# Two of four weight sums by accumulating DMAs in a Strassen MLP, with four weight buffers and operands read back unsplit

## The chip, the cores and the metric

The kernel runs on one core of a Trainium2 chip. The metric is the device time of one execution in microseconds. The core has a matrix engine (TensorE, PE in the profile), VectorE (DVE), ScalarE (ACT), GpSimd (POOL) and a queue engine (SyncE, SP); DMAs are issued from SP, ACT and POOL and run on 16 DMA engines.

## The reference, cut to what matters

One layer of a hybrid encoder for 512 tokens of width 2048: an input projection, two attention mixers and an output projection, a cross attention to 256 memory tokens, and an MLP. The change is in the MLP and the final norm behind it:

```python
hm = rmsnorm(x, g_mlp[l])                                     # x: 512 x 2048
x = x + jnp.square(jax.nn.relu(hm @ w_up[l])) @ w_down[l]     # w_up: 2048 x 8192, w_down: 8192 x 2048
return rmsnorm(x, g_final)
```

## The kernel before

Everything is float32, split for the matrix engine into a high and a low part (`hi_lo`: ACT casts to float32r, DVE subtracts), so that a product is three matmuls: high by high, high by low, low by high.

**Units.** The two MLP products are cut into 256 units, 128 of up and then 128 of down. A unit is one block of 256 by 512 weights, used as four 128 x 256 pieces a21, a12, a11, a22 in one 128 x 1024 row, against a pair of operand blocks. It is done with Strassen's scheme (Winograd's form): seven products in place of eight. The seven left operands are the three pieces a12, a11, a22 and four sums of pieces; the seven right operands are three blocks of the activations and four sums. Seven products, two halves, three matmuls each: 42 matmuls of 128 x 256 columns a unit (line 310). Eight units that add up in the same seven PSUM banks are a group (up: one g of 16) or a visit (down: one ng for one c, 16 in all); then the seven banks are combined by `gen_up_out` or `gen_down_out`. There are eight banks, so the next group can begin in the one that is free and goes on as the others are released.

**A unit's weights** (`loader`, `strassen_split`, L1450). SP loads the row into one of three `wraw` buffers. POOL forms the four sums in `sring`: one instruction of 512 columns and two of 256. Once the unit two back has been through the matrix engine, `hi_lo` writes the 768 loaded and then the 1024 summed columns into one of two buffers of tile `hl`.

**Up.** The right operands of the eight pairs lie split in tile `big` (`gen_xpair`; the sums of pairs 2 to 7 are made on POOL). At a group's end `gen_up_out` combines the banks on DVE and ACT, applies relu, square and the norm's factor, forms the sums on DVE (four of 512 columns), splits all 3584 columns (two casts of 1792 on ACT, two subtractions of 1792 on DVE) and stores high and low parts from ACT's queue to `tp_dram`: four DMAs of 896 KB.

**Down.** Four chunks c of eight operand pairs, each chunk used by the four ng in turn. `gen_load_t` loads a split pair (1792 KB, ACT's queue) into one of the eight places of `big` when the last visit of the previous chunk has used it, so all eight of a chunk change within one visit. `gen_down_out` adds a visit's banks to the four residual tiles of its ng, part of it on POOL. In the last chunk `gen_square` sums squares in `acc_f` on POOL, and `gen_out` ends the kernel.

**Order of the work.** Each engine runs its own queue in order. The order is fixed at build time by a planner (`Plan`): generators (`spawn`, `until`) issue an instruction when the planner's estimated clocks say that its inputs are ready. All engine instructions of these helpers carry line 139, so they are told apart by tile and shape: on DVE `hl<-wraw,hl 128x768` and `hl<-fb,hl 128x1024` are the two subtractions of a unit's split, on POOL `fb<-wraw 128x512` and `fb<-fb,wraw 128x256` are its sums.

Of the kernel before, what the change touches and what calls it, by code (L numbers as in the profile page):

```python
# [33 lines left out]
FW = 49 * 256  # L34
# [124 lines left out]
def kernel(  # L159
# [32 lines left out]
    wraw = [cp.tile([128, 1024], F32, name=f"wraw{i}") for i in range(3)]  # L192
# [6 lines left out]
    acc_f = cp.tile([128, 512], F32, name="acc_f")  # L199
# [3 lines left out]
    tp_dram = nc.dram_tensor("tp_dram", (32, 128, PAIR), F32, kind="Internal").ap()  # L203
# [5 lines left out]
    cosT = cp.tile([128, 4, 32], F32, name="cosT")  # L209
    sinT = cp.tile([128, 4, 32], F32, name="sinT")  # L210
# [1143 lines left out]
    PRODUCTS = {"p1": (0, 0), "p2": (2, 1), "q4": (1, 6), "p7": (3, 5), "q5": (4, 3), "q6": (5, 4), "p3": (6, 2)}  # L1354
    ORDER = ("p1", "p2", "q4", "p7", "q5", "q6", "p3")
    LAST_ORDER = ("p1", "q6", "p7", "q4", "p2", "q5", "p3")
# [3 lines left out]
    sring = [fslot(4096 + 1024 * i, 1024) for i in range(2)]  # L1360
    gxbufs = Pool([fslot(10496, 2048)])
# [16 lines left out]
    def residual1(n, b):  # L1378

        yield rt(b, res[n])  # L1380
        dve.tensor_tensor(res[n], res[n], b, op=OP.add)
        banks_f.put(b)
        flag.add(("x1", n))
        if n % 2:
            spawn(gen_xpair(n // 2), True)
        yield rt(res[n])
        nc.sync.dma_start(xs_dram[n], res[n])
        while n > 0 and ("sq", 1, n - 1) not in flag:
            yield 0
# [15 lines left out]
    def gen_xpair(q):  # L1405
# [12 lines left out]
        sums([c(4), c(5), c(6), c(7)], c(0), c(1), c(2), c(3), dve if q < 2 else pool)  # L1418
# [6 lines left out]
        flag.add(("xp", q))  # L1425
        if q == 3:
            while not all(("sq", 1, n) in flag for n in range(8)):
                yield 0
            gxbufs.put(fslot(6144, 2048))
# [19 lines left out]

    def strassen_split(i):  # L1450

        raw, s = wraw[i % 3], sring[i % 2]
        hi, lo = HI[units[i].buf], LO[units[i].buf]
        while i == first_s and not all(("xp", q) in flag and ("sq", 1, 2 * q + 1) in flag for q in range(2)):
            yield 0
        while not splits[i - 2].done:
            yield 0
        yield rt(raw)
        two = lambda x: x.rearrange("p (u c) -> p u c", u=2)
        a21 = raw[:, 0:256]  # L1460
# [8 lines left out]
    def strassen_pe(buf, st, pair, first, last, order):  # L1469

        hi, lo = HI[buf], LO[buf]
        for r in order:
            w, t = PRODUCTS[r]
            if first:
                st[r] = take_now(banks_f)[0]
            th, tl = pair[:, 256 * t : 256 * t + 256], pair[:, 1792 + 256 * t : 2048 + 256 * t]
            for e in range(2):
# [4 lines left out]
                smm(out, lo[:, c], th, False, last)  # L1482

    G = fslot(0, 4096)
    HT = fb[:, 6144 : 6144 + 3584].bitcast(F32R)
    CT = fslot(10496, 2048)

    def gen_up_out(g, st):
# [3 lines left out]
        while g == 0 and len(gxbufs) < 2:  # L1492
            yield 0
        while g > 0 and ("t", g - 1) not in flag:
            yield 0
        yield rt(st["p1"])
        act.copy(e1, st["p1"])
        banks_f.put(st["p1"])
        yield rt(e1, st["p2"])
        dve.tensor_tensor(c11, e1, st["p2"], op=OP.add)  # L1500
        banks_f.put(st["p2"])
        yield rt(st["q5"])
        act.copy(e5, st["q5"])
# [31 lines left out]
        for a in (0, 1792):  # L1535
            src = G[:, 512 + a : 2304 + a]
            yield from hi_lo(HT[:, a : a + 1792], src.bitcast(F32R), src)
        for x, o in ((HT.bitcast(F32), 0), (G[:, 512:4096], 1792)):
            yield rt(x)
            for m in range(2):  # L1540
                dst = tp_dram[2 * g + 1 - m][:, o : o + 1792].rearrange("p (r c) -> p r c", r=7)
                nc.scalar.dma_start(dst, x.rearrange("p (r m c) -> p r m c", r=7, m=2)[:, :, m, :])
        flag.add(("t", g))

    def up_units(g):
        st = {}

        def pe(kk):
            def run(buf):
# [12 lines left out]
    def gen_load_t(p):  # L1562

        yield plan.clk["pe"]
        while ("t", p // 2) not in flag:
            yield 0
        dst = big[:, PAIR * (p % 8) : PAIR * (p % 8) + PAIR]
        nc.scalar.dma_start(dst.bitcast(F32), tp_dram[p])
        plan.issue("dma", 100.0, [dst], [], 7000)
        TP[p] = dst  # L1570


    CB = [[[fslot(o + 1024 * m + 512 * t) for t in range(2)] for m in range(2)]
          for o in (0, 2048, 6144, 8192)]
    ev = Pool([fslot(10496 + 512 * i) for i in range(3)])
# [15 lines left out]
    def gen_down_out(c, ng, st, last):  # L1591
# [3 lines left out]
        e1, u2, u3 = yield from take(ev, 3)  # L1595
        side = dve if last else pool
        yield rt(st["p1"])
        act.copy(e1, st["p1"])
        banks_f.put(st["p1"])

        def add(dst, r, op, free=True):
            dve.tensor_tensor(dst, dst, st[r], op=op)
            if free:
                banks_f.put(st[r])

        if last:
            yield rt(st["q6"], e1)
            dve.tensor_tensor(u2, e1, st["q6"], op=OP.subtract)
            banks_f.put(st["q6"])
            side.tensor_tensor(c12, c12, u2, op=OP.add)  # L1610
            yield rt(st["p7"], u2)
            dve.tensor_tensor(u3, u2, st["p7"], op=OP.add)
            banks_f.put(st["p7"])
            side.tensor_tensor(c21, c21, u3, op=OP.subtract)
            side.tensor_tensor(c22, c22, u3, op=OP.subtract)
            yield rt(st["q4"])
            add(c21, "q4", OP.subtract)
            flag.add(("fin", ng, 1, 0))
            side.tensor_tensor(c11, c11, e1, op=OP.add)
            yield rt(st["p2"])  # L1620
            add(c11, "p2", OP.add)
            flag.add(("fin", ng, 0, 0))
            yield rt(st["q5"])
            add(c22, "q5", OP.add, False)
            flag.add(("fin", ng, 1, 1))
            add(c12, "q5", OP.subtract)
            yield rt(st["p3"])
            add(c12, "p3", OP.add)
            flag.add(("fin", ng, 0, 1))
        else:  # L1630
            yield rt(st["p2"], e1)
            add(c11, "p2", OP.add)
            side.tensor_tensor(c11, c11, e1, op=OP.add)
            yield rt(st["q5"])
            add(c12, "q5", OP.subtract, False)
            add(c22, "q5", OP.add)
            yield rt(st["q6"])
            dve.tensor_tensor(u2, e1, st["q6"], op=OP.subtract)
            banks_f.put(st["q6"])
            dve.tensor_tensor(u3, u2, st["p7"], op=OP.add)  # L1640
            banks_f.put(st["p7"])
            add(c21, "q4", OP.subtract)
            yield rt(st["p3"])
            add(c12, "p3", OP.add)
            side.tensor_tensor(c12, c12, u2, op=OP.add)
            side.tensor_tensor(c21, c21, u3, op=OP.subtract)
            side.tensor_tensor(c22, c22, u3, op=OP.subtract)
            for m in range(2):
                for t in range(2):
                    flag.add(("fin", ng, m, t))  # L1650
        ev.put(e1, u2, u3)
# [6 lines left out]
    def down_units(c, ng):  # L1658
        st = {}
        end = c == 3 and ng == 3  # L1660

        def pe(j):
            def run(buf):
                p = 8 * c + j
                if c == 0 and ng == 0 and j == 0:
# [330 lines left out]
```

## Time and profile before

| what | us |
|---|---|
| median of 3 runs | 2441.43 (2439.35 to 2444.55) |
| the profiled execution, its own time | 2439.85 |
| span of its profile | 2438.0 |
| first matmul of the MLP (line 310) | 948.8 |
| last matmul of the MLP | 2409.1 |

The profiled execution is 1.58 us under the median and its own time is 1.85 us over its span. Times below are from the span's start. Busy time is by engine; DMA share is the mean of the 16 DMA engines.

### The profile page before, as it was taken

Reading aid. Unit: us, or ns where it says so; the run is one execution under the profiler, and the core shown is the slowest. Engines: PE = TensorE matmul, PEld = TensorE weight load, DVE = VectorE, ACT = ScalarE, POOL = GpSimd, SP = SyncE. Lnnn points to the kernel's source line nnn. Section 1 sums busy time; section 2 is a strip of 40 time slices with the busy share of each in tenths; the row PEclk is TensorE's granted clock in tenths of the full one; section 3 lists DMA queues with packets and bytes.
Section 4 is the critical chain, followed back from the end, with each engine's and each line's share of the span. In section 5 each row is a group of like instructions: output and inputs, shape, how many; then the busy total and the mean of one; then the engine's idle time right before and its main releaser. Section 6 shows DMA issues by size and latency. Waiting matters only on the chain.

```text
span 2438.0 us, 39899 instructions
## 1 busy us (share of the span) xinstructions
PE 2275.2 (93%) x16024; PEld 2182.4 (90%) x16024; DVE 1683.8 (69%) x2018; ACT 1056.9 (43%) x1481; POOL 1385.2 (57%) x1078
## 2 busy tenths in 40 slices
PE   8999999999999998799999999999799999999995
PEld 8999999998888887799899899898799999999984
DVE  7678434458633667788988988887666666676656
ACT  6543333345432555545545545444333333333432
POOL 3110101021011107888778787786698998998994
PEclk9999999999999999899999999999899999999997
DMA  5332222231343434164464464468737338347322
GB/s 169 102 91 85 72 78 78 68 104 36 104 172 110 154 127 146 61 212 168 149 214 156 163 206 151 166 204 326 263 97 305 136 113 328 113 145 289 103 79 87
DMA packets 144090, 361.45 MB, mean 148 GB/s; under 512 B 10241, under 2 KB 75793, under 8 KB 139553
## 3 DMA queue, kind: packets, MB, share of 16 engines
q1 hardware_dynamic: 79072, 239.76, 29.6%
q10 hardware_dynamic: 64752, 119.06, 13.4%
q8 instruction: 125, 2.05, 0.4%
q14 instruction: 61, 0.49, 0.1%
q0 software_dynamic: 80, 0.08, 0.0%
HBM read 291.76 MB, written 67.11 MB: 147 GB/s over the span
## 4 chain that ended last, share of the span: by engine, by line
PE 45%; POOL 26%; DVE 14%; issue 8%; DMA 5%; ACT 1%; SPq 0%; DVEq 0%; ACTq 0%; POOLq 0%
PE bank L305 30%; POOL fb L139 26%; PE bank L310 14%; DVE fb L139 8%; DVE hl L139 4%; DMA wraw<-in_w_dn_dram 4%; PE bank L330 2%; DVE big L139 1%; DMA wraw<-in_w_up_dram 1%; ACT hl L139 0%; POOL acc_f L139 0%; DMA tp_dram<-fb 0%; DMA fb<-xs_dram 0%; ACT fb L139 0%; DVE small L139 0%
## 5 line engine op out<-in xcount | busy, mean ns | idle before, releaser
L310 PE MATMUL bank<-big,hl 128*128 128x256 f32 x10752 | 1339.1, 287 | 103.0 <-DVE hl L139 73.4
L310 PEld LDWEIGHTS bank<-big,hl 128*128 128x128 f32 x10752 | 1323.3, 196 | 118.4 <-DVE hl L139 84.3
L139 DVE TENSOR_TENSOR hl<-wraw,hl 128x768 fp32r<-128x768 f32 (+4 forms) x442 | 568.6, 1287 | 330.8 <-ACT hl L139 329.8
L139 POOL TENSOR_TENSOR fb<-fb,wraw 128x256 f32<-128x256 f32 x512 | 671.9, 1312 | 40.1
L139 DVE TENSOR_TENSOR hl<-fb,hl 128x1024 fp32r<-128x1024 f32 x256 | 390.1, 1524 | 297.2 <-ACT hl L139 278.4
L139 ACT CAST hl<-wraw 128x768 fp32r<-128x768 f32 (+4 forms) x442 | 378.9, 858 | 464.9 <-PE bank L305 289.8
L305 PE MATMUL bank<-hl,big 128*128 128x384 f32 (+4 forms) x2916 | 525.0, 330 | 7.5 <-ACT big L139 6.5
L139 ACT CAST hl<-fb 128x1024 fp32r<-128x1024 f32 (+1 forms) x257 | 269.1, 1047 | 560.9 <-POOL fb L139 483.0
L139 POOL TENSOR_TENSOR fb<-wraw 128x512 f32<-128x512 f32 x256 | 414.7, 1620 | 171.6 <-DVE hl L139 117.8
L305 PEld LDWEIGHTS bank<-hl,big 128*128 128x128 f32 x2916 | 479.2, 189 | 18.5 <-ACT big L139 6.5
L139 POOL TENSOR_TENSOR fb<-fb 128x512 f32<-128x512 f32 (+4 forms) x175 | 225.3, 1308 | 301.0 <-ACT fb L139 195.8
L305 PE MATMUL bank<-big,hl 128*128 128x512 f32 (+1 forms) x1192 | 296.1, 390 | 0.0
L305 PEld LDWEIGHTS bank<-big,hl 128*128 128x128 f32 x1192 | 222.2, 188 | 43.3
L139 DVE TENSOR_TENSOR fb<-fb 128x512 f32<-128x512 f32 (+4 forms) x207 | 254.3, 1255 | 4.6 <-ACT fb L139 3.8
L139 POOL TENSOR_TENSOR fb<-fb,cosT 128x128 f32<-128x128 f32 (+3 forms) x48 | 26.8, 558 | 389.9 <-DVE fb L139 308.1
L139 ACT ACTIVATE fb<-fb 128x512 f32<-128x512 f32 (+3 forms) x142 | 115.7, 820 | 85.1 <-POOL fb L139 31.8
L139 DVE TENSOR_TENSOR fb<-fb,bank 128x512 f32<-128x512 f32 x208 | 136.2, 680 | 10.3 <-PE bank L310 5.9
L305 PE MATMUL bank<-big 128*128 128x256 f32 (+2 forms) x534 | 113.2, 327 | 2.1 <-DVE big L139 1.2
L305 PEld LDWEIGHTS bank<-big 128*128 128x128 f32 x534 | 87.1, 188 | 10.1 <-DVE big L139 2.5
L139 ACT CAST big<-bank 128x512 fp32r<-128x512 f32 (+2 forms) x119 | 61.2, 540 | 56.5 <-PE bank L330 28.4
L139 POOL TENSOR_TENSOR small<-small,nhalf 128x4 f32<-128x4 f32 (+1 forms) x7 | 8.4, 1204 | 134.0 <-DVE small L139 133.9
L139 ACT CAST fb<-fb 128x1792 fp32r<-128x1792 f32 (+2 forms) x58 | 63.6, 1100 | 47.4 <-DVE fb L139 44.5
(97 smaller groups left out, 911.7 us busy)
## 6 DMA issues: line engine op xcount, KB each, us to landing
wraw<-in_w_up_dram SPq DMA_DIRECT2D x128, 512.0 KB, 3.6
wraw<-in_w_dn_dram SPq DMA_DIRECT2D x128, 512.0 KB, 3.4
tp_dram<-fb ACTq DMA_DIRECT2D x64, 896.0 KB, 7.3
big<-tp_dram ACTq DMA_DIRECT2D x32, 1792.0 KB, 11.5
wraw<-in_w_in_dram SPq DMA_DIRECT2D x80, 384.0 KB, 3.0
wraw<-in_w_out_dram SPq DMA_DIRECT2D x32, 512.0 KB, 3.4
fb<-in_xT_dram SPq DMA_DIRECT2D x16, 256.0 KB, 4.4
wraw<-in_w_in_dram SPq DMA_DIRECT2D x16, 256.0 KB, 2.6
```

The costliest lines, as they stand in the source:

```text
L139: r = fn(*args, **kw)
L305: nc.tensor.matmul(out, lhsT, rhs, start=start, stop=stop)
L310: nc.tensor.matmul(out, lhsT, rhs, start=start, stop=stop, skip_group_check=True)
L330: nc.tensor.transpose(out, in_, ident)
```

## The change

- **Weights.** Four buffers (`ring`) of 1792 columns, in the unit's order of the seven left operands, replace three `wraw` and two `sring` in the MLP. SP loads a12 and a11 into blocks 0 and 5 (two runs of 1 KB a partition) and a12, a11, a22 into blocks 2 to 4 (one run of 3 KB). Then an accumulating DMA from POOL adds a21, read twice from DRAM, onto blocks 0 and 5. DVE forms the other two sums (two instructions of 256). A buffer is loaded again when the split of the unit four back is done.
- **Split.** Columns 0 to 1023 are split once the unit two back has done four of its seven products, the rest when it has done all seven; the matmuls of a unit's first four products start behind the first part. The order of the seven products is the same everywhere, and each bank's combination is issued behind its own last product.
- **Operands of down.** `gen_up_out` stores the unsplit 3584 columns from SP's queue (two DMAs of 896 KB a group, no split). `gen_load_t` loads an unsplit pair (896 KB, SP's queue) and splits it on ACT and DVE. A visit v uses pairs 2v to 2v+7 (mod 32), so two pairs are loaded for each visit, 38 in all.
- **Smaller moves.** `gen_down_out` is on DVE alone (11 instructions of 512 columns) with one buffer; `gen_xpair` has one buffer and all its sums on DVE; `wraw`, `cosT`, `sinT` and `acc_f` move into tile `fb`, which grows from 49 to 64 blocks of 256 columns.

```diff
-FW = 49 * 256
+FW = 64 * 256
-    tp_dram = nc.dram_tensor("tp_dram", (32, 128, PAIR), F32, kind="Internal").ap()
+    tp_dram = nc.dram_tensor("tp_dram", (32, 128, 1792), F32, kind="Internal").ap()
-    ORDER = ("p1", "p2", "q4", "p7", "q5", "q6", "p3")
+    PRODUCTS = {"p1": (2, 0), "q6": (1, 4), "p7": (0, 5), "q4": (3, 6), "p2": (4, 1), "q5": (5, 3), "p3": (6, 2)}
+    ORDER = tuple(PRODUCTS)
-    sring = [fslot(4096 + 1024 * i, 1024) for i in range(2)]
-    gxbufs = Pool([fslot(10496, 2048)])
+    ring = [fslot(o, 1792) for o in (4096, 5888, 7680, 13568)]
+    gxbufs = Pool([fslot(11264, 2048)])
...
-        sums([c(4), c(5), c(6), c(7)], c(0), c(1), c(2), c(3), dve if q < 2 else pool)
+        flag.add(("xg", q))
+        sums([c(4), c(5), c(6), c(7)], c(0), c(1), c(2), c(3), dve)
...
+    def load_blocks(i):
+        k = i - first_s
+        if k == 0:
+            need = lambda: all(("xg", q) in flag for q in range(2)) and ("sq", 1, 3) in flag
+        elif k < 3:
+            need = lambda: all(("xg", q) in flag for q in range(4)) and ("sq", 1, 7) in flag
+        elif k == 3:
+            need = lambda: first_s - 2 in splits and splits[first_s - 2].done
+        else:
+            need = lambda: i - 4 in splits and splits[i - 4].done
+        while not need():
+            yield 0
+        r, src = ring[k % 4], units[i].src
+        s31 = bass_blocks(r, 0, 5)
+        nc.sync.dma_start(s31, src[:, 256:768].rearrange("p (u c) -> p u c", u=2))
+        plan.issue("dma", 700.0, [r[:, 0:256], r[:, 1280:1536]], [], 2600)
+        nc.sync.dma_start(r[:, 512:1280], src[:, 256:1024])
+        plan.issue("dma", 1000.0, [r[:, 512:1280]], [], 2600)
+
+        def add_a21():
+            yield rt(r[:, 0:256], r[:, 1280:1536])
+            a21 = src[:, 0:256].unsqueeze(1).to_broadcast([128, 2, 256])
+            nc.gpsimd.dma_start(s31, a21, accum_op=OP.add)
+            plan.issue("pool", 1000.0, [r[:, 0:256], r[:, 1280:1536]], [], 3000)
+            flag.add(("load", i))
+        spawn(add_a21(), True)
...
     def strassen_split(i):
-        pool.tensor_tensor(two(s[:, 0:512]), two(raw[:, 256:768]), a21.unsqueeze(1).to_broadcast([128, 2, 256]), op=OP.add)
-        pool.tensor_tensor(s[:, 512:768], s[:, 256:512], raw[:, 256:512], op=OP.add)
-        pool.tensor_tensor(s[:, 768:1024], s[:, 512:768], raw[:, 768:1024], op=OP.add)
-        while ("pe", i - 2) not in flag:
-            yield 0
-        yield from hi_lo(hi[:, 0:768], lo[:, 0:768], raw[:, 256:1024])
-        yield from hi_lo(hi[:, 768:1792], lo[:, 768:1792], s)
+        r, hi, lo = ring[(i - first_s) % 4], HI[units[i].buf], LO[units[i].buf]
+        c = lambda j: r[:, 256 * j : 256 * j + 256]
+        yield rt(r)
+        dve.tensor_tensor(c(1), c(5), c(2), op=OP.add)
+        dve.tensor_tensor(c(6), c(1), c(4), op=OP.add)
+        while ("pa", i - 2) not in flag:
+            yield 0
+        yield from hi_lo(hi[:, 0:1024], lo[:, 0:1024], r[:, 0:1024])
+        flag.add(("sa", i))
+        while ("pe", i - 2) not in flag:
+            yield 0
+        yield from hi_lo(hi[:, 1024:1792], lo[:, 1024:1792], r[:, 1024:1792])
...
     def gen_up_out(g, st):
-        for a in (0, 1792):
-            src = G[:, 512 + a : 2304 + a]
-            yield from hi_lo(HT[:, a : a + 1792], src.bitcast(F32R), src)
-        for x, o in ((HT.bitcast(F32), 0), (G[:, 512:4096], 1792)):
-            yield rt(x)
-            for m in range(2):
-                dst = tp_dram[2 * g + 1 - m][:, o : o + 1792].rearrange("p (r c) -> p r c", r=7)
-                nc.scalar.dma_start(dst, x.rearrange("p (r m c) -> p r m c", r=7, m=2)[:, :, m, :])
+        yield rt(G)
+        x = G[:, 512:4096].rearrange("p (r m c) -> p r m c", r=7, m=2)
+        for m in range(2):
+            nc.sync.dma_start(tp_dram[2 * g + 1 - m].rearrange("p (r c) -> p r c", r=7), x[:, :, m, :])
...
-    def gen_load_t(p):
+    NLOAD = 38
+    def gen_load_t(s):
+        p = s % 32
...
-        dst = big[:, PAIR * (p % 8) : PAIR * (p % 8) + PAIR]
-        nc.scalar.dma_start(dst.bitcast(F32), tp_dram[p])
+        dst = big[:, PAIR * (s % 8) : PAIR * (s % 8) + PAIR]
+        hi, lo = dst[:, 0:1792], dst[:, 1792:3584]
+        src = lo.bitcast(F32)
+        nc.sync.dma_start(src, tp_dram[p])
+        yield from hi_lo(hi, lo, src)
+        TP[s] = dst
...
-    def gen_down_out(c, ng, st, last):
+    def gen_down_out(ng, st):
+        def add(dst, x, op=OP.add):
+            dve.tensor_tensor(dst, dst, x, op=op)
...
-    for c in range(4):
-        for ng in range(4):
-            units.extend(down_units(c, ng))
+    for v in range(16):
+        units.extend(down_units(v))
```

## Rows read from the trace of the kernel before

**Rows 1.** The page: busy time of each engine over the span.

```profile
PE 2275.2 (93%) x16024; PEld 2182.4 (90%) x16024; DVE 1683.8 (69%) x2018; ACT 1056.9 (43%) x1481; POOL 1385.2 (57%) x1078
```

**Rows 2.** Windows: us, busy us (instructions) by engine, granted clock, DMA share.

```profile
948.50:1018.30 69.80, 48.35 (x350) 46.75 (x350) 44.12 (x33) 33.73 (x47) 66.41 (x52) 0.83 0.23 76
1018.30:1700.70 682.40, 625.33 (x5043) 618.42 (x5042) 589.97 (x465) 343.35 (x359) 538.54 (x359) 0.98 0.55 187
1700.70:1803.90 103.20, 87.54 (x674) 85.48 (x673) 70.19 (x56) 37.98 (x42) 77.59 (x55) 0.92 0.61 216
1803.90:1884.80 80.90, 80.90 (x675) 80.74 (x674) 55.41 (x43) 28.55 (x32) 74.54 (x54) 1.00 0.61 232
1884.80:2409.20 524.40, 499.53 (x4034) 494.31 (x4032) 335.21 (x281) 189.86 (x222) 477.28 (x355) 0.98 0.43 157
2409.20:2438.00 28.80, 3.34 (x14) 2.57 (x12) 20.04 (x26) 3.10 (x5) 10.62 (x7) 0.55 0.44 146
```

**Rows 3.** A window inside one group of eight up units.

```profile
1310.40:1324.60 14.20, 11.98 (x100) 11.78 (x99) 12.49 (x8) 4.30 (x5) 12.45 (x8) 1.00 1.03 359
```

**Rows 4.** Lines by shape, 1018.3 to 1700.7: busy us, mean ns, idle.

```profile
L139 POOL TENSOR_TENSOR fb<-fb,wraw 128x256 f32<-128x256 f32 x239 | 326.8, 1367 | 18.7
L139 POOL TENSOR_TENSOR fb<-wraw 128x512 f32<-128x512 f32 x120 | 214.2, 1785 | 125.1 <-DVE hl L139 110.7 <-DMA wraw<-in_w_up_dram 11.4 <-DMA wraw<-in_w_dn_dram 2.8
L139 DVE TENSOR_TENSOR hl<-fb,hl 128x1024 fp32r<-128x1024 f32 x120 | 184.2, 1535 | 80.1 <-ACT hl L139 73.3 <-PE bank L310 6.8
L139 DVE TENSOR_TENSOR hl<-wraw,hl 128x768 fp32r<-128x768 f32 x120 | 162.5, 1354 | 8.5 <-ACT hl L139 8.3
...
L139 DVE TENSOR_TENSOR fb<-fb 128x512 f32<-128x512 f32 x90 | 94.8, 1092 | 0.5
L139 DVE TENSOR_TENSOR fb<-fb 128x1792 fp32r<-128x1792 f32 x30 | 75.7, 2561 | 0.0
...
L139 DVE TENSOR_TENSOR fb<-fb 128x1024 f32<-128x1024 f32 x30 | 44.5, 1485 | 0.0
L139 DVE TENSOR_TENSOR fb<-fb,bank 128x512 f32<-128x512 f32 x60 | 40.8, 681 | 2.4 <-PE bank L310 1.8
```

**Rows 5.** Waits, 1018 to 1700: who waited for whom, us, times, longest.

```profile
PE bank L310 <- DVE hl L139: 56.6, 33, 2.3
```

**Rows 6.** Instructions on tile hl, 1018 to 1700: ns min/median/max.

```profile
L139 DVE TENSOR_TENSOR hl<-wraw,hl x120: 943/1474/2067, 1018.2 to 1695.4; 128x768 fp32r<-128x768 f32 x120
...
L139 DVE TENSOR_TENSOR hl<-fb,hl x120: 1209/1257/2319, 1023.5 to 1698.6; 128x1024 fp32r<-128x1024 f32 x120
```

**Rows 7.** DVE on tile fb, same stretch: ns min/median/max.

```profile
L139 DVE TENSOR_TENSOR fb<-fb x150: 676/1225/3117, 1021.7 to 1672.2; 128x512 f32<-128x512 f32 x90, 128x1024 f32<-128x1024 f32 x30, 128x1792 fp32r<-128x1792 f32 x30
```

**Rows 8.** Lines by shape, 1804 to 2219 (down).

```profile
L139 DVE TENSOR_TENSOR hl<-wraw,hl 128x768 fp32r<-128x768 f32 x79 | 125.8, 1592 | 0.6 <-ACT hl L139 0.5
L139 DVE TENSOR_TENSOR hl<-fb,hl 128x1024 fp32r<-128x1024 f32 x79 | 117.7, 1490 | 135.3 <-ACT hl L139 135.3
```

**Rows 9.** Instructions on tile acc_f: ns min/median/max.

```profile
L139 DVE TENSOR_TENSOR acc_f<-acc_f,fb x8: 416/424/426, 2413.2 to 2416.4; 128x256 f32<-128x256 f32 x8
```

**Rows 10.** DMA queues in 1300 to 1400: packets, MB, share of 16 engines.

```profile
q1 hardware_dynamic: 2560, 9.31, 27.2%
q10 hardware_dynamic: 7519, 7.57, 23.0%
```

**Rows 11.** DMA issues over the span: KB each, median us to landing.

```profile
wraw<-in_w_up_dram SPq DMA_DIRECT2D x128, 512.0 KB, 3.6
...
cs<-in_cst_dram POOLq DMA_DIRECT2D x1, 80.0 KB, 4.7
```

**Rows 12.** Instructions on tile cs: ns min/median/max.

```profile
L430 POOL DMA_DIRECT2D cs<-in_cst_dram x1: 747/747/747, 1.3 to 1.3; - x1
```

**Rows 13.** Timeline at the change from up to down: start, us, [idle].

```profile
1738.57 9.40 SPq L1586 DMA_DIRECT2D fb<-xs_dram  x15
...
1756.03 1.26 POOL L139 TENSOR_TENSOR fb<-wraw 128x512 f32<-128x512 f32 x1 [15.76 <-DMA wraw<-in_w_dn_dram]
```

More of the change, by code (lines that the diff above doesn't have):

```diff
@@ L191 @@
     bank = [psp.tile([128, 512], F32, name=f"bank{i}") for i in range(8)]
-    wraw = [cp.tile([128, 1024], F32, name=f"wraw{i}") for i in range(3)]
     hl = cp.tile([128, 2 * PAIR], F32R, name="hl")
@@ L1464, in strassen_split, with strassen_pe @@
         while ("pe", i - 2) not in flag:
             yield 0
-        yield from hi_lo(hi[:, 0:768], lo[:, 0:768], raw[:, 256:1024])
-        yield from hi_lo(hi[:, 768:1792], lo[:, 768:1792], s)
-    def strassen_pe(buf, st, pair, first, last, order):
-        hi, lo = HI[buf], LO[buf]
-        for r in order:
+        yield from hi_lo(hi[:, 1024:1792], lo[:, 1024:1792], r[:, 1024:1792])
+    def strassen_pe(i, st, pair, first, last):
+        hi, lo = HI[units[i].buf], LO[units[i].buf]
+        until(lambda: ("sa", i) in flag)
+        for x, r in enumerate(ORDER):
@@ L1473, in strassen_pe @@
             w, t = PRODUCTS[r]
+            if x == 4:
+                flag.add(("pa", i))
+                until(lambda: splits[i].done)
             if first:
@@ L1482, in strassen_pe, with product @@
                 smm(out, lo[:, c], th, False, last)
+            if last:
+                flag.add((id(st), r))
+    def product(st, r):
+        while (id(st), r) not in flag:
+            yield 0
+        yield rt(st[r])
     G = fslot(0, 4096)
-    HT = fb[:, 6144 : 6144 + 3584].bitcast(F32R)
-    CT = fslot(10496, 2048)
+    CT = fslot(11264, 2048)
     def gen_up_out(g, st):
@@ L1491, in gen_up_out @@
         c11, c21, c12, c22 = (CT[:, 512 * i : 512 * i + 512] for i in range(4))
-        while g == 0 and len(gxbufs) < 2:
+        while g == 0 and not all(q in XP for q in range(8)):
             yield 0
@@ L1548, in pe, with run @@
         def pe(kk):
-            def run(buf):
+            def run(i):
                 if g == 0 and kk == 0:
@@ L1594, in gen_down_out @@
             yield 0
[L1595 to L1650, printed above, removed]
@@ L1651, in gen_down_out, with free @@
-        ev.put(e1, u2, u3)
+        e = (yield from take(ev))[0]
+        def add(dst, x, op=OP.add):
+            dve.tensor_tensor(dst, dst, x, op=op)
+        def free(r):
+            banks_f.put(st[r])
+        yield from product(st, "p1")
+        act.copy(e, st["p1"])
+        free("p1")
+        yield from product(st, "q6")
+        yield rt(e)
+        add(c11, e)
+        add(e, st["q6"], OP.subtract)
+        free("q6")
+        yield from product(st, "p7")
+        add(c12, e)
+        add(e, st["p7"])
@@ new lines, in gen_down_out @@
+        free("p7")
+        add(c21, e, OP.subtract)
+        yield from product(st, "q4")
+        add(c21, st["q4"], OP.subtract)
+        free("q4")
+        flag.add(("fin", id(st), 1, 0))
+        add(c22, e, OP.subtract)
+        ev.put(e)
+        yield from product(st, "p2")
+        add(c11, st["p2"])
+        free("p2")
+        flag.add(("fin", id(st), 0, 0))
+        yield from product(st, "q5")
+        add(c22, st["q5"])
+        flag.add(("fin", id(st), 1, 1))
+        add(c12, st["q5"], OP.subtract)
@@ L1653, in down_index @@
+        free("q5")
+        yield from product(st, "p3")
+        add(c12, st["p3"])
+        free("p3")
+        flag.add(("fin", id(st), 0, 1))
     def down_index(p, ng):
@@ L1686, in gen_square @@
             x = CB[ng][m][t]
-            while ("fin", ng, m, t) not in flag or (ng > 0 and ("sqd", ng - 1) not in flag):
+            while ("fin", id(st), m, t) not in flag or (ng > 0 and ("sqd", ng - 1) not in flag):
                 yield 0
             yield rt(x)
-            s = (yield from take(sq_f if ng < 3 else sq_l))[0]
+            s = (yield from take(ev if ng < 3 else sq_l))[0]
             act.activation(s, x, AF.Square)
@@ L1867, in splitter, with ensure @@
             n = u.n
-            yield from hi_lo(whi[u.buf][:, 0:n], wlo[u.buf][:, 0:n], wraw[i % 3][:, 0:n])
+            yield from hi_lo(whi[u.buf][:, 0:n], wlo[u.buf][:, 0:n], wraw[u.buf][:, 0:n])
+    def ensure(i):
+        if i < nu and i not in splits:
+            splits[i] = spawn(splitter(i), True)
     spawn(loader())
-    for i in range(2):
-        splits[i] = spawn(splitter(i), True)
+    ensure(0)
+    ensure(1)
     for i in range(nu):
-        if i + 2 < nu:
-            splits[i + 2] = spawn(splitter(i + 2), True)
+        ensure(i + 2)
+        if i + 3 >= first_s:
+            ensure(i + 3)
         if i == 3:
@@ L1881 @@
             plan.mlp = True
-        until(lambda: splits[i].done)
         if i < first_s:
+            until(lambda: splits[i].done)
             units[i].pe(whi[units[i].buf], wlo[units[i].buf])
+            flag.add(("pa", i))
         else:
-            units[i].pe(units[i].buf)
+            units[i].pe(i)
         flag.add(("pe", i))
```

126 lines of the change are left out of this document (63 added, 63 removed).

## The prediction, made before any run of the changed kernel

> **What bounds the kernel now.** I read the page first: PE is busy 93% of the span, VectorE 69%, POOL 57% [rows 1]. The table of windows says where PE is not fed [rows 2]. From 1803.9 to 1884.8 PE has no idle time at full clock: 675 matmuls in 80.90 us, 119.9 ns each, so a unit of 42 takes 5.03 us. That is PE's floor, and the change leaves the 42 matmuls alone. 256 units need 1288 us; the MLP takes 1460.7 (948.5 to 2409.2). The missing 173 us, stretch by stretch against 40.2 us for eight units: the first group 69.8, 29.6 over; up's groups 1 to 15 682.4, 78.8 over (5.3 a group); two visits at the turn from up to down 103.2, 22.7 over; the next two 0.4 over; the last twelve 524.4, 41.5 over.
>
> In up the loss lies in the middle of each group: in 1310.4 to 1324.6 PE is busy 11.98 of 14.20 us and DVE 12.49 [rows 3]. The table of waits names the last releaser: PE waits 56.6 us for the split on DVE, 33 times [rows 5]. DVE is busy 590.0 of 682.4 us, POOL 538.5 [rows 2]. The two lean on each other: POOL's first sum waits 110.7 us for DVE to leave its buffer [rows 4], and DVE runs slower beside POOL: the same 128x768 subtraction takes 943 to 2067 ns, mean 1354 [rows 4, 6]. At the turn one weight load keeps POOL idle for 15.76 us, behind 15 residual loads on SP that wait for the last store [rows 13].
>
> **The change, part by part.**
>
> *POOL's sums go.* A unit loses 1.785 + 2 x 1.367 = 4.52 us on POOL [rows 4]. In their place POOL issues one accumulating DMA. The nearest row is a plain one of 128 rows, 0.75 us of POOL [rows 12]; 256 runs make 1.5, with a second read each perhaps 3 as an estimate from it. Either fits in 5.03.
>
> *DVE in up, a group.* If DVE runs at its fastest rows: splits 0.943 + 1.209 [rows 6], two new sums at 0.424 [rows 9], together 3.00 a unit, 24.0 for eight; five PSUM instructions at 0.681, six of 512 columns at 0.676, two of 1024 at 1.209 [rows 4, 6, 7], 9.9 together. The two subtractions of 1792, 5.1 us in a row [rows 4], are gone. Sum 33.9 of 40.2 us. If DVE keeps its means of today [rows 4], it is 3.74 a unit, 29.9, plus 3.4 + 6.6 + 3.0: 42.9, over PE's 40.2. I take the fast rows, since POOL's arithmetic is what goes.
>
> Here the Trainium skill has a rule (SBUF — State Buffer, Who interferes with whom): a DVE instruction with two SBUF inputs contends with a GpSimd instruction that reads SBUF, and not with one that only writes it. By it the split of 943 ns returns as POOL stops reading, and the sum is the 33.9; the spread of rows 6 agrees with a contention, but no row shows DVE beside POOL issuing DMAs back to back.
>
> *DVE in down, a visit.* 24.0 for splits and sums, 11 combinations at 0.68, 7.5, and two subtractions of 1792: 1.209 + 768 x 1.04 ns (the slope between rows 6) is 2.01 each, 4.0. Sum 35.5 of 40.2. With today's means [rows 8], 3.93 a unit: 31.4 + 7.5 + 2 x 2.56 [rows 4] = 44.1.
>
> *DMA.* In 1300 to 1400 the 1 KB packets of q10 take 0.230 x 1600 / 7519 = 48.9 ns of an engine, and q1 moves 9.31 MB in 435 us of engines, 21.4 GB/s each [rows 10]. A unit's 256 runs of 1 KB cost 0.78 us of all 16, its 393 KB in rows of 3 KB 1.15, the group's store (1792 packets) 5.48, 0.68 a unit; in down two loads of 918 KB 5.4 a visit, 0.67 a unit. That is 2.6 before the accumulation. The trace has no accumulation. From below its 256 runs cost 0.78, if they went like a copy. From above the nearest row is far: POOL's one larger DMA before, 80 KB, lands 4.7 us after its issue [rows 11], 0.75 of which is POOL's [rows 12]; if all the rest were engine time, 262 KB would take some 12.7 us. I take a value near the lower end, two copies, 1.56, because a landing is mostly waiting (a 512 KB load lands in 3.6 us [rows 11], though 21.4 GB/s an engine makes 1.5 of it), and because each run is read from DRAM and its old value from SBUF: 4.2 us in 5.03. The DMA engines become PE's pace at 3.1 copies (2.4 us) and eat the whole gain, 5.6 us a unit, at 3.9.
>
> The Trainium skill (Collectives: The Full Stack, The bandwidth ceiling) says that adding in a DMA engine halves its rate, not through the add but through two source reads, and gives 62.28 against 32.35 GB/s. That would be 1.93 copies, 1.5 us, and the sum would stand.
>
> *Waits added.* POOL's accumulation waits for SP's block load; behind it stand the next unit's accumulation and, in the last visits, the sums of squares. DVE's two sums wait for the accumulation, with the combinations that release PE's banks behind them: a late accumulation stops PE twice. The way to a unit's split is 3.6 us for the load, 1.5 to 3 for POOL's issue, some 4.7 to land [rows 11], 0.85 for the sums: 11 to 12 us. A buffer is released about half a unit before its own unit starts on PE, and its next unit's first part can be split some 2.5 units after that start: three units, 15 us. So 3 to 4 us are spare, and I cost the latency at nothing; without that cover it is its excess once per late unit. Splitting behind the fourth product gives back half a unit of room. The 32 stores and 38 pair loads stand on SP now, before on ACT's queue: a store waits for DVE's last sums and a pair load for PE to leave its place in `big`, with the weight loads behind them. The planner puts them where it expects them ready, and a delay of up to the 3 to 4 us stays hidden.
>
> *By stretch.* Up's groups: the run of 1792s in the middle is gone and DVE has 6 us a group to spare; I leave 1 us each, 16 for 78.8 (0 to 78.8). First group: POOL's 66.4 busy of 69.8 [rows 2] goes, but DVE takes the pairs' sums (16 at 0.42 for four pairs) with one buffer: 16 for 29.6 (5 to 35). Turn: the same residual loads stand on SP, against half the stored and loaded bytes and one buffer more: 10 for 22.7 (0 to 25). Down: the bursts of eight loads at each chunk and POOL's sums beside the squares go, but DVE has 7.5 us of combinations and 4.0 of operand splits in the first three units of a visit, beside 9.0 of their own splits, in 15 to 17 us: 1.6 a visit, 22 for 41.9 (5 to 60). Before the MLP, 948.5, and the tail, 28.8 [rows 2], stay.
>
> Sum: 948.5 + 1288 + 16 + 16 + 10 + 22 + 28.8 = 2329.3 span. The profiled execution's own time is 1.85 above its span, and the median 1.58 above that: **2333 us**.
>
> **The rivals.**
> 1. *DVE becomes the bound*: it stays as slow beside POOL's DMA issue as beside POOL's sums. Up 16 x 42.9 = 686, down 16 x 44.1 = 706, first group and turn 26, with 977.3 around them: 2395, 2399 as a median. For it: nothing shows how descriptor writing treats DVE. Against: POOL would be issuing under 3 of 5 us.
> 2. *Slower*: an accumulated run costs more than 3.9 copies (191 ns). At six, 293 ns, a unit is 2.6 + 4.7 = 7.3 us: 1869 + 977 + 26, 2875. For it: no row excludes it, and 1 KB runs are short. Against: q10 writes 1 KB runs at 20.6 GB/s an engine, hardly under q1's rate.
> 3. *Accumulation between 3.1 and 3.9 copies*: it binds, at 5.03 to 5.6 us a unit: 2333 to 2440.
> 4. *The gain is not there*: the latency of load, POOL and accumulation exceeds the ring's 15 us, say by 5 us once a half group. 32 x 5 = 160 is more than the loss removed: near 2440. Against: three to four us are spare.
>
> **How the numbers follow.** Forecast 0.60, own range 2295 to 2375 (the low end: 5, 0, 0 and 5 us left in the four stretches give 2279; all four at once I hold for rare). Rival 1: 0.13. Rival 2: 0.12. Rival 3: 0.08. Rival 4: 0.07, half of it slower. About 0.2%, 5 us, is what a measurement can tell. Faster: 0.60 + 0.13 + 0.07 from rival 3 and 0.01 from rival 4, 0.81; the same 0.04; slower 0.15. The range runs from 2295 to 2435: rival 2, most of rival 4 and little at the low end stay out.
>
> **What would show it.** Right: matmuls at 119.9 ns through whole groups; no POOL arithmetic in up; DVE's 768-column split near 0.95 us and its busy share near 84% in up, 88% in down; software DMA packets under 100 ns; PE's waits left at the first three units of a visit. Wrong: DVE's mean split still 1.35 (rival 1); DMA share at 1.0 throughout with DVE waiting for the accumulation (rivals 2 and 3); DVE waiting for it with a DMA share well under 1 (rival 4).

## The result, and the profile after the change

The changed kernel takes 2523.43 us (median of 4 runs, 2512.15 to 2528.44), the kernel before 2442.99 beside it: a ratio of 1.0323, 95% interval 1.0285 to 1.0361. It is slower by 80 us; 2333 was forecast. The profiled execution of after is the fastest of the four, 2512.15 us with a span of 2510.4, so 11 of the 80 us stand in no row below.

The page of after, busy time by engine; it answers to [rows 1]:

```profile
PE 2306.0 (92%) x16024; PEld 2200.6 (88%) x16024; DVE 1676.5 (67%) x2620; ACT 1074.4 (43%) x1487; POOL 483.9 (19%) x482
```

POOL's weight sums are gone, VectorE is no busier than before, and PE is still not fed. The windows of after, cut at the first matmul of the first group, of up's groups 1 to 15, of the first two visits and of the other fourteen, and then the first unit of one group of up and its other seven (columns as in [rows 2]):

```profile
954.40:1017.20 62.80, 47.75 (x349) 46.73 (x350) 53.56 (x74) 34.49 (x47) 21.12 (x17) 0.86 0.61 150
1017.20:1701.90 684.70, 636.34 (x5043) 628.95 (x5042) 482.46 (x673) 306.58 (x336) 143.28 (x119) 0.96 0.80 210
1701.90:1812.60 110.70, 86.86 (x673) 84.22 (x673) 76.65 (x99) 44.82 (x46) 19.25 (x16) 0.92 0.85 237
1812.60:2480.60 668.00, 601.17 (x4706) 583.93 (x4704) 471.05 (x626) 264.91 (x279) 154.27 (x131) 0.97 0.71 186
...
1234.70:1246.00 11.30, 7.93 (x45) 7.53 (x44) 8.63 (x15) 4.48 (x7) 2.41 (x2) 0.70 0.52 133
1246.00:1282.00 36.00, 35.53 (x296) 35.32 (x296) 25.07 (x35) 15.96 (x18) 7.22 (x6) 1.00 0.88 229
```

The last two rows show one of the longer groups: one unit of 11.3 us, then units at 5.04 us (296 matmuls at 120 ns). Up's groups 1 to 15 take 40.3 to 55.0 us, and the late unit is mostly the first, the second or the last; in visits 2 to 15 it is the first each time, 9.1 to 14.3 us. What each stretch takes over 40.32 us for eight units (the columns of before and of the forecast are the prediction's, over 40.2):

| stretch | over, before | forecast | over, after |
|---|---|---|---|
| first group | 29.6 | 16 | 22.5 |
| up, groups 1 to 15 | 78.8 | 16 | 79.9 |
| turn (visits 0 and 1) | 22.7 | 10 | 30.1 |
| visits 2 to 15 | 41.9 | 22 | 103.5 |

So up gained nothing, and down lost some 60 us. The first matmul of the MLP comes at 954.4 for 948.8 before, where the forecast had no change. The waits say at whose hands (columns as in [rows 5]): the first lines are of 1018 to 1700, those behind the dots of 1812 to 2480.

```profile
DVE fb L139 <- DMA fb<-in_w_up_dram: 184.8, 85, 7.1
...
PE bank L308 <- DVE hl L139: 29.3, 21, 3.7
...
PE bank L308 <- DVE fb L139: 18.7, 9, 3.3
...
DVE fb L139 <- DMA fb<-in_w_dn_dram: 141.0, 51, 5.2
...
PE bank L308 <- DVE fb L139: 55.8, 55, 4.7
```

PE waits for VectorE as in [rows 5], but VectorE now waits for DMA. (`DVE hl` is the split of a unit, `DVE fb` here a combination that frees a bank: in up PE waits longer for splits, in down for banks.) The timeline at the start of a visit (start, us, engine and instruction, idle before and its releaser) shows how the one becomes the other:

```profile
1992.70 1.20 POOL L1468 DMA_DIRECT2D fb<-in_w_dn_dram  x1 [0.44 <-DVE hl L139]
...
2000.46 0.88 DVE L139 TENSOR_TENSOR fb<-fb 128x256 f32<-128x256 f32 x2 [2.27 <-DMA fb<-in_w_dn_dram]
2001.26 0.95 DVE L139 TENSOR_TENSOR hl<-fb,hl 128x768 fp32r<-128x768 f32 x1
2002.13 0.68 DVE L139 TENSOR_TENSOR fb<-fb 128x512 f32<-128x512 f32 x1
...
2002.92 0.69 DVE L139 TENSOR_TENSOR fb<-fb,bank 128x512 f32<-128x512 f32 x1
...
2003.66 1.65 PE L308 MATMUL bank<-big,hl 128*128 128x256 f32 x6 [3.97 <-DVE fb L139]
```

The accumulation of 1992.70 has not landed when VectorE comes to that unit's two sums. It stands still for 2.27 us, then does the sums and a split, and only at 2002.13 begins the combinations of the visit before. (A visit's first bank is copied out by ACT, so `gen_down_out` is not on DVE alone.) The combination of 2002.92 is the first that reads a bank, and PE, which has waited 3.97 us for one, goes on when it is done. The chain of waits puts the piece at the DMA:

```profile
1992.70 7.73 DMA fb<-in_w_dn_dram
```

The DMA view of 1018 to 1700 (queue: packets, MB, share of 16 engines; then issues as in [rows 11]):

```profile
q0 software_dynamic: 32398, 31.23, 30.9%
...
fb<-in_w_up_dram SPq DMA_DIRECT2D x115, 384.0 KB, 5.1
fb<-in_w_up_dram POOLq DMA_DIRECT2D x116, 256.0 KB, 6.0
fb<-in_w_up_dram SPq DMA_DIRECT2D x115, 256.0 KB, 4.0
tp_dram<-fb SPq DMA_DIRECT2D x30, 896.0 KB, 8.8
```

An accumulation follows its 256 KB load: 4.0 + 6.0 = 10.0 us from SP's issue to sums that can start. The planner, which writes VectorE's queue, has 700 + 2600 ns for that load, 1000 + 2600 for the other and 1000 + 3000 for the accumulation (lines 1461 to 1469): 7.3 us. So, at the medians, it sets the two sums into the queue some 2.7 us ahead of their data.

### The profile page after: what moved, and what is told of

It reads as the page before. It is cut to its first block, busy times and chain, and to the rows that moved or that the text cites. A ratio compares the mean times of both kernels' runs of the same rounds, so it can differ in the third digit from the quotient of the medians.

```text
span 2510.4 us, 40561 instructions
## 1 busy us (share of the span) xinstructions
PE 2306.0 (92%) x16024; PEld 2200.6 (88%) x16024; DVE 1676.5 (67%) x2620; ACT 1074.4 (43%) x1487; POOL 483.9 (19%) x482
## 4 chain that ended last, share of the span: by engine, by line
PE 38%; DMA 29%; DVE 22%; issue 6%; POOL 3%; ACT 1%; DVEq 0%; POOLq 0%; SPq 0%; ACTq 0%
PE bank L303 29%; DMA fb<-in_w_up_dram 16%; DMA fb<-in_w_dn_dram 13%; DVE fb L139 10%; DVE hl L139 8%; PE bank L308 7%; DVE big L139 3%; POOL fb L139 2%; PE bank L328 2%; ACT fb L139 1%; ACT hl L139 1%; DMA big<-tp_dram 0%; POOL fb L1468 0%; DMA fb<-in_w_in_dram 0%; DVE small L139 0%
## 5 line engine op out<-in xcount | busy, mean ns | idle before, releaser
L139 ACT CAST hl<-fb 128x768 fp32r<-128x768 f32 (+4 forms) x699 | 645.2, 927 | 1046.6 <-PE bank L308 478.2
L139 DVE TENSOR_TENSOR hl<-fb,hl 128x768 fp32r<-128x768 f32 (+4 forms) x698 | 744.9, 1083 | 330.0 <-ACT hl L139 329.4
L139 DVE TENSOR_TENSOR fb<-fb 128x256 f32<-128x256 f32 (+3 forms) x779 | 405.0, 528 | 387.2 <-DMA fb<-in_w_up_dram 191.7
L139 POOL TENSOR_TENSOR fb<-fb 128x128 f32<-128x128 f32 (+5 forms) x209 | 165.7, 814 | 706.9 <-ACT fb L139 378.2
L1468 POOL DMA_DIRECT2D fb<-in_w_dn_dram x128 | 154.1, 1205 | 597.0 <-DMA fb<-in_w_dn_dram 223.9
L1468 POOL DMA_DIRECT2D fb<-in_w_up_dram x128 | 154.3, 1212 | 559.1 <-DMA fb<-in_w_up_dram 263.3
L139 ACT ACTIVATE fb<-fb 128x512 f32<-128x512 f32 (+2 forms) x144 | 116.5, 813 | 141.5 <-DVE fb L139 118.0
L303 PEld LDWEIGHTS bank<-big 128*128 128x128 f32 x534 | 87.1, 189 | 10.1 <-DVE big L139 2.5
L139 DVE TENSOR_TENSOR big<-bank,big 128x512 fp32r<-128x512 f32 (+1 forms) x102 | 62.8, 643 | 25.5 <-ACT big L139 25.4
L139 DVE TENSOR_TENSOR big<-big 128x1792 fp32r<-128x1792 f32 x38 | 76.7, 2019 | 0.4 <-ACT big L139 0.4
L139 ACT CAST big<-big 128x1792 fp32r<-128x1792 f32 x38 | 64.3, 1691 | 20.9 <-DMA big<-tp_dram 20.8
```

The lines of the kernel that those rows point to most:

```text
L139: r = fn(*args, **kw)
L303: nc.tensor.matmul(out, lhsT, rhs, start=start, stop=stop)
L1468: nc.gpsimd.dma_start(s31, a21, accum_op=OP.add)
```

## The experiments

Theory: what costs most of the 190 us between forecast and time is the place of the two sums in VectorE's queue, set by a delay that is too short. Rivals: the accumulation's own path is too long wherever it stands (rival 4 of the prediction); VectorE's new work, in bursts, is what PE waits for. Each ratio is to the kernel before on the same chip.

| run | median, us | ratio (95%) |
|---|---|---|
| after | 2523.43 | 1.0323 (1.0285 to 1.0361) |
| e1_lags | 2422.62 | 0.9918 (0.9888 to 0.9948) |
| e2_no_a21 | 2325.33 | 0.9519 (0.9503 to 0.9535) |
| e3_pool_two | 2453.2 | 1.0035 (1.0021 to 1.0048) |
| e4_dve_four | 2385.45 | 0.977 (0.9755 to 0.9786) |
| e5_long_lag | 2416.86 | 0.9898 (0.9879 to 0.9918) |
| e6_dve_four_turn | 2379.77 | 0.974 (0.9724 to 0.9757) |
| e7_dve_four_short_lag | 2387.03 | 0.9777 (0.976 to 0.9794) |
| e9_no_stores | 2368.65 | 0.9699 (0.9684 to 0.9715) |
| e10_stores_act | 2386.63 | 0.9768 (0.9751 to 0.9784) |
| e11_dve_four_turn_act | 2372.35 | 0.97 (0.9686 to 0.9714) |
| e12_stores_loads_act | 2398.26 | 0.9805 (0.9788 to 0.9822) |
| e13_dve_four_loads_act | 2373.76 | 0.9702 (0.9687 to 0.9718) |

**The planned delays alone (e1), and a still longer one (e5).** The engines' work and the DMAs are the same; only their places in the queues move.

```diff
-        plan.issue("dma", 700.0, [...], [], 2600)
+        plan.issue("dma", 700.0, [...], [], 3400)
-        plan.issue("dma", 1000.0, [...], [], 2600)
+        plan.issue("dma", 1000.0, [...], [], 4000)
-            plan.issue("pool", 1000.0, [...], [], 3000)
+            plan.issue("pool", 1200.0, [...], [], 4800)   # e5: 6800
```

> Only the delays that the planner assumes for a weight load and for the accumulating DMA are raised to what the changed kernel's trace shows (block load 3.3 to 4.1 us from issue, the 3 KB rows 3.6 to 5.0, the accumulation 4.0 to 6.0); that moves instructions in the queues and nothing else. Order theory (VectorE's two weight sums stand in its queue before their accumulation has landed, and the combinations that release PE's banks stand behind them): PE's 4 to 9 us at the first unit of a visit go in most visits, 2350 to 2430 us. Path theory (load, accumulation, sums and split take longer than four buffers allow, whatever the order): the wait moves from the banks to the splits, 2500 to 2540 us.

> As the run with the trace's delays, but the planner takes the accumulation to land 8.0 us after its issue, over every median of the traces (5.4 to 6.3). If the 2 to 4 us that are left at the first unit of a group are still VectorE's queue order, they shrink and it is 2370 to 2410 us; if they are the way through load and accumulation itself (path theory for the rest), it stays within 2405 to 2440.

Four numbers of the plan, three delays and the length of POOL's issue, give back 101 us. The windows of e1, up's groups 1 to 15 and visits 2 to 15:

```profile
1007.40:1667.20 659.80, 622.55 (x5042) 613.68 (x5041) 480.10 (x674) 301.58 (x335) 143.29 (x119) 0.99 0.83 217
1784.40:2395.60 611.20, 579.71 (x4705) 574.32 (x4704) 474.12 (x623) 265.18 (x279) 151.36 (x130) 0.98 0.78 202
```

55.0 us are over in up (79.9 after) and 46.7 in visits 2 to 15 (103.5 after). The waits of e1, the first two of 1018 to 1700, the last of 1812 to 2390:

```profile
PE bank L308 <- DVE hl L139: 41.6, 22, 4.7
...
PE bank L308 <- DVE fb L139: 4.8, 11, 0.6
...
PE bank L308 <- DVE fb L139: 29.2, 21, 3.1
```

PE's wait for banks falls in both (18.7 to 4.8, 55.8 to 29.2), but in up its wait for splits rises (29.3 to 41.6), the sign that was named for the path theory. So the order was the larger part, and down's above all. In e5 the late unit of a group of up moves from the first to the third; up has 69.9 over, down 26.5. The whole gains 6 us, which is not clear of the spread of the runs (2413.71 to 2422.29 against 2414.77 to 2430.53). So in up a later place gives nothing back and the rest is a path; in down 20 of e1's 46.7 us were order still.

**No accumulation (e2).** The a21 block is missing from the sums; all else as in e1.

```diff
-            nc.gpsimd.dma_start(s31, a21, accum_op=OP.add)
-            plan.issue("pool", 1000.0, [...], [], 3000)
```

> The accumulating DMA is left out, so a21 is missing from the four sums; loads, VectorE's sums, splits and combinations stay, with the load delays of the trace in the planner. Order and path theory both: the late thing is gone, and what is left is VectorE's bursts, the first group and the turn from up to down, 2330 to 2390 us. Third theory (VectorE's eleven combinations and four more instructions per unit are too much at a visit's start by themselves): PE still loses 3 us or more at the first unit of nearly every visit, over 2430 us.

The windows of e2, the same two stretches:

```profile
1007.80:1612.60 604.80, 604.80 (x5043) 604.80 (x5042) 482.60 (x673) 308.70 (x335) 0.00 (x0) 1.00 0.55 185
1719.10:2293.10 574.00, 567.93 (x4706) 565.09 (x4704) 469.48 (x621) 266.35 (x279) 23.22 (x22) 1.00 0.47 165
```

Up has no PE idle time at all, with VectorE's work all there (482.6 us, as after). The theory of VectorE's bursts falls. 2325 is 5 us under the expected range and within 8 us of the forecast: the forecast was about the time of this kernel with the accumulation for nothing. Its terms fit less well than their sum: 18.5, 0, 25.9 and 9.5 us are over in the four stretches, where 16, 16, 10 and 22 were forecast.

**The same sums without the accumulation: on POOL (e3), on VectorE (e4; e7 with the change's short delays for the loads).** The a21 block comes by a third plain load, into the free block 6 of the buffer; one instruction of 512 columns adds it. The delays for the loads are e1's, except in e7.

```diff
+        nc.sync.dma_start(r[:, 1536:1792], src[:, 0:256])
...
-            nc.gpsimd.dma_start(s31, a21, accum_op=OP.add)
+            pool.tensor_tensor(v, v, a21, op=OP.add)   # e4, e7: dve.tensor_tensor
```

> The accumulating DMA is replaced by a plain load of a21 (128 KB more from SP, into block 6) and one POOL addition of 512 columns per unit; VectorE keeps its two sums. Measured load delays in the planner. Order and path theory: the way is shorter by the 5.4 to 6 us of the accumulation less 1.3 to 1.8 for POOL, so the first units' loss goes; VectorE is slowed beside POOL for a third of the time: 2340 to 2400 us. Third theory: over 2430.

> As the run with POOL's addition, but VectorE does it (0.68 us a unit), so VectorE makes all four sums and POOL none. By the rows VectorE then has 39.3 us of work a group in up and 41 a visit in down against PE's 40.3: it is the bound, 2370 to 2440 us. If VectorE's bursts already cost the changed kernel its gain (third theory), it is worse than 2523.

> As the run in which VectorE makes all four sums, but the planner takes loads to land 2.6 us behind its queue's clock, as in the changed kernel (3.4 and 4.0 before). Order theory: plain loads land near that, so little hangs on it, 2380 to 2410 us. If any misjudged delay costs as much as in the changed kernel, over 2420.

e3 misses its expectation: over 2430 was to speak for VectorE's bursts, but e2 and e4, with as much work on VectorE or more, do not bear them out. The lines by shape of e3, 1018 to 1640, and behind the dots two of after, 1018 to 1700:

```profile
L139 POOL TENSOR_TENSOR fb<-fb 128x512 f32<-128x512 f32 x111 | 167.1, 1505 | 456.3 <-DMA fb<-in_w_up_dram 399.2 <-DVE fb L139 46.6 <-DVE hl L139 10.6
L139 DVE TENSOR_TENSOR hl<-fb,hl 128x1024 fp32r<-128x1024 f32 x111 | 150.8, 1359 | 2.0 <-ACT hl L139 2.0
L139 DVE TENSOR_TENSOR hl<-fb,hl 128x768 fp32r<-128x768 f32 x112 | 142.8, 1275 | 0.7 <-ACT hl L139 0.7
...
L139 DVE TENSOR_TENSOR hl<-fb,hl 128x1024 fp32r<-128x1024 f32 x119 | 145.1, 1219 | 1.9 <-ACT hl L139 1.9
L139 DVE TENSOR_TENSOR hl<-fb,hl 128x768 fp32r<-128x768 f32 x119 | 113.3, 952 | 1.4 <-ACT hl L139 1.4
```

With 1.5 us of POOL arithmetic a unit back, VectorE's splits are at 1275 and 1359 ns, toward [rows 4]; in after they are at 952 and 1219. The Trainium skill (SBUF — State Buffer, Who interferes with whom) has VectorE with two SBUF inputs contend with a GpSimd instruction that reads SBUF; the trace agrees in both directions. VectorE also waits 90.4 us for POOL's sum in this stretch; how e3's loss divides between the two was not told apart. e4 is 58 us faster than the kernel before. e7 equals e4: with these plain loads, delays planned about a microsecond shorter cost nothing. So in e1 it was probably the accumulation's delay that counted; its numbers were not changed one by one.

**Where up's rest comes from: no operand stores (e9), and the stores on ACT's queue (e10).** Both from e1. e9 stores the operands of the first group only, and the pair loads read those.

```diff
-        for m in range(2):
+        for m in range(2 if g == 0 else 0):          # e9
...
-            nc.sync.dma_start(tp_dram[2 * g + 1 - m]...
+            nc.scalar.dma_start(tp_dram[2 * g + 1 - m]...   # e10
```

> As the run with the trace's delays, but only the first group's operands are stored to DRAM, and all loads of down read those, so that 15 groups' stores of 2 x 896 KB are missing and the output is not the reference's. If up's rest of 2 to 4 us a group comes from the stores' packets beside load and accumulation at a group's end, up's groups fall to 40.3 to 41 us and it is 2380 to 2395 us; if it is the accumulation's own length, up stays and it is 2410 to 2425.

> The kernel with the longer planned delays, and the 32 operand stores issued on ACT's queue as the kernel before did, in place of SP's. What the run without stores left open is how the stores cost up its rest of 2 to 4 us a group. Theory A: the weight loads stand behind the store's 1792 packets in SP's ring (the two loads after a store are issued in 1.87 and 1.69 us in place of 0.38 and 0.47); then another ring gives most of it back, up groups 40.3 to 42, 2375 to 2395 us. Theory B: the packets take the DMA engines' time beside load and accumulation, whichever queue they come from; then up groups stay at 42 to 46, 2410 to 2430 us.

e9 makes 13 of up's groups 1 to 15 40.3 us (the others 46.0 and 41.0). It is faster than expected, since the turn is shorter too (25.5 us over, 36.6 in e1). e10 keeps every byte of the stores and gives back 36 of e1's us by the queue alone. The timeline of SP in e1, around a store:

```profile
1288.93 0.47 SPq L1462 DMA_DIRECT2D fb<-in_w_up_dram  x1
1289.44 1.23 SPq L1586 DMA_DIRECT2D tp_dram<-fb  x2
1292.24 1.87 SPq L1460 DMA_DIRECT2D fb<-in_w_up_dram  x1
1294.15 1.69 SPq L1462 DMA_DIRECT2D fb<-in_w_up_dram  x1
```

The two weight loads behind the store are issued in 1.87 and 1.69 us in place of 0.38 and 0.47, and land 10.1 and 9.2 us after their issue, where the medians are 3.9 and 5.2. The windows of e10, up's groups 1 to 15 and visits 2 to 15:

```profile
1008.20:1629.90 621.70, 610.30 (x5043) 607.42 (x5042) 481.43 (x674) 304.94 (x335) 143.34 (x119) 1.00 0.87 230
1739.20:2356.80 617.60, 583.07 (x4705) 577.45 (x4704) 477.61 (x625) 265.85 (x279) 152.48 (x131) 0.98 0.77 201
```

16.9 us are over in up, where 16 were forecast. The same bytes now move in less time, and the DMA engines are busier for it than in e1 (0.87 against 0.83), so it was not their capacity.

**The turn, and the fastest version (e6, e11).** e6 is e4 with the 16 residual loads (line 1640) on `nc.gpsimd`; e11 is e6 with the stores on `nc.scalar`.

> As the run in which VectorE makes all four sums, but the 16 residual loads at the turn from up to down go out from POOL's queue, not from SP's. If they hold up the weight loads on SP (one load 20 us late in that run), some 15 to 25 us of the turn's 34 go: 2360 to 2372 us. If the transfers themselves keep the DMA engines from the weights, within 5 us of 2385.

> The fastest version so far (all four sums on VectorE from three plain loads, residual loads on POOL's queue) with the stores on ACT's queue. Here no accumulation follows a load, so the store delays only one load; up groups are 40.3 to 44 us with the stores on SP, 26.8 us over in fifteen groups. Theory A: 2360 to 2372 us. Theory B: 2376 to 2384 us, as without the move.

e6 gains about 6 us of an expected 15 to 25: a unit of 20.33 us in visit 0 becomes 5.04, but the next visit's first grows from 8.01 to 12.14. e11, at 2372.35, is the fastest version of the study that does all the work; it lies between its two theories and decides neither.

**The pair loads on ACT's queue (e12 from e10, e13 from e11).**

```diff
-        nc.sync.dma_start(src, tp_dram[p])
+        nc.scalar.dma_start(src, tp_dram[p])
```

> The kernel with longer planned delays and the stores on ACT's queue, and now the 38 pair loads of 896 KB on ACT's queue too, so that SP's ring holds weight loads alone in both halves. Theory A (down's rest is, as up's, weight loads standing behind 896 KB in SP's ring): visits of 41.8 to 47.4 us come to 41 to 43, 2355 to 2372 us. Theory B (down's rest is the accumulation's own length and DVE's run of combinations, with the bank waits of 32 us that visits show): visits stay, 2380 to 2392 us; a pair load that waits on ACT for its place could then cost a few us more.

> The fastest version so far (four sums on VectorE, residual loads on POOL's queue, stores on ACT's) with the pair loads on ACT's queue too. Visits are 42.4 to 43.9 us with 2.1 of it at the first unit, where DVE does eight combinations of 0.68 us beside sums and splits; no run shows that these wait for a load. Theory A: 2355 to 2366 us. Theory B: 2368 to 2378 us.

e13 equals e11, and e12 is 12 us slower than e10, more than either of its theories has; why was not looked into. Down's rest is not a weight load behind a pair load on SP.

## Why the prediction was wrong

**The step that failed** is in "Waits added": "So 3 to 4 us are spare, and I cost the latency at nothing". The length of the way was right: 11 to 12 us forecast, 4.0 + 6.0 + 0.9 = 10.9 measured at the medians (a single accumulation takes up to 10.6). The spare time was counted in the ring of buffers, where it exists: groups 2 to 5 of e10 run at 40.3 us with all their accumulations. It does not exist in VectorE's queue, which executes in order: there the sums stand where the planner expected them, 7.3 us behind the load, and whatever is behind them waits, the bank-freeing combinations too. The same paragraph names that consequence ("a late accumulation stops PE twice") and prices it at nothing. The planner's 7.3 us can be added up from the diff, and the prediction itself has 9.8 to 11.3 us for the same way (3.6, 1.5 to 3, and 4.7); setting one against the other was the missing step. e1 shows its price: 101 of the 190 us between forecast and time.

**The second step**, "a delay of up to the 3 to 4 us stays hidden" for the stores and pair loads on SP, failed for the stores: SP issues a group's two in 1.23 us, but the loads behind them in the same queue come some 4 to 6 us late. That is 36 us (e1 to e10). For the pair loads the runs show no such cost (e12, e13). Of the 54 us that e10 still lies over the forecast, 31 are in visits 2 to 15 and 19 at the turn.

**The rivals.** Rival 4, given 0.07, is the nearest: VectorE waits for the accumulation with a DMA share of 0.71 to 0.80. Its mechanism, though, was the ring and not the queue's order, and its price, 5 us a half group (near 2440), was short; after loses 64 us more than forecast in up and 82 in visits 2 to 15. (It does not follow from rival 4's own numbers either: its 160 us on top of 2333 would be 2493.) Rivals 2 and 3 fall: the accumulated 1 KB packet takes 0.309 x 16 x 682 us / 32398 = 104 ns, 2.1 of the 48.9 ns copies of [rows 10], where two were taken and 3.1 were needed to bind. The Trainium skill (Collectives: The Full Stack, The bandwidth ceiling) gives a measured 1.93 between its copying and its adding collective; the trace's 2.1 is a tenth above that. Rival 1 falls: VectorE's 768-column split is at 952 ns.

**What held.** PE's 5.03 us a unit (5.04). VectorE 482.5 us in fifteen groups, 32.2 each (33.9 forecast), and 33.6 a visit (35.5). POOL's issue is cheaper than forecast, 1.20 us (1.5 to 3). Up comes to 16.9 over once the order and the stores' queue are mended (e10), but by luck: the forecast's 16 stood for VectorE, and without the accumulation VectorE costs up nothing (e2). First group: 22.5 for 16, inside its bounds.

**The turn** was forecast at 10, and is 30.1. The timeline of after:

```profile
1741.65 17.34 SPq L1640 DMA_DIRECT2D fb<-xs_dram  x16
...
1765.88 1.20 POOL L1468 DMA_DIRECT2D fb<-in_w_dn_dram  x1 [21.11 <-DMA fb<-in_w_dn_dram]
...
1770.88 0.88 DVE L139 TENSOR_TENSOR fb<-fb 128x256 f32<-128x256 f32 x2 [11.34 <-DMA fb<-in_w_dn_dram]
...
1774.15 6.03 PE L308 MATMUL bank<-big,hl 128*128 128x256 f32 x35 [13.06 <-DVE fb L139]
```

The residual loads hold SP for 17.34 us, 5.12 of which SP waits, behind the first of them, until the last store has landed. That is no more than before: there all 16 hold it for 18.74 us, from 1729.23, with 8.11 of such a wait, and [rows 13] begins behind it. The weight loads come behind them as before, but now the accumulation adds its 5 us to that. Half the stored bytes and one buffer more did not outweigh it. Even without the accumulation 25.9 are over (e2), and with SP freed of these loads 24.6 (e6, for 34.1 in e4), so SP is not the whole of it; what else holds the turn was not isolated.

**Left open.** Down's rest with the accumulation in its right place: 53.1 us over in visits 2 to 15 of e10, 9.5 without the accumulation (e2). It is the accumulation's, and PE's waits there are for VectorE's bank-freeing combinations (32.2 us, 24 times, in 1750 to 2356 of e10). Some of it is order: e5's longer delay brings visits 2 to 15 from 46.7 over in e1 to 26.5. How much is the length of the DMA was not told apart, and e5's delay was not run together with the stores on ACT's queue.

## What to carry to other kernels

When a sum moves from an engine to a DMA, look first at what stands behind its consumer in an in-order queue, and compare the delay that the schedule assumes with the trace's time from issue to landing, not with the DMA engines' busy share: here the planned times of three DMAs were worth 101 us at the same work. A large store does not have to be waited for to do harm: put it on another queue than the loads that feed the critical engine. And where one more load and one VectorE instruction fit, they beat the accumulating DMA here (e4 is 37 us ahead of e1, both with the stores on SP; e11 is 14 ahead of e10, both with them on ACT's queue, some 6 of it by the residual loads' move). With a delay as long as e5's, and the stores on ACT's queue, the accumulation might do better than in e10; that was not run.

## What the runs showed of the hardware that was not expected

- The pauses of PE cost more than their own length. In the row 1234.70:1246.00 PE stands 3.3 us; behind that the granted clock is at the lower of its two levels (0.50, 1.2 GHz, over 25 matmuls in 5.30 us from 1239.9) and then at the upper again (1.00, 2.4 GHz). The row's 45 matmuls take 7.93 us, where 45 x 119.9 ns is 5.40. In up of after, 48.4 us are waits (684.7 - 636.3) and 31.7 slower matmuls (636.3 - 5043 x 0.1199).
- Behind a 1.75 MB store on SP's queue, SP needed 1.87 and 1.69 us to issue loads that take 0.38 and 0.47; with the store on ACT's queue the up stretch went from 659.8 to 621.7 us at the same bytes.
- An accumulating DMA of 256 runs of 1 KB lands 5.8 us after its issue (median of 244; 4.5 to 10.6) and the loads beside it are slower: the 384 KB load lands in 5.1 us, in e2, without accumulations, in 3.9.
- SP's 17.34 us on the 16 residual loads are not all issue: one load of 256 KB is issued in 0.47 us (median; 0.36 to 2.10), some 10 us for the 16, and 5.12 are one wait for a store to land.
